# A feed-forward kernel with a gated GELU: transposes moved among the last products of a group, and the last product split by token halves

## The chip, the cores and the metric

One core of a Trainium2 chip. Its engines work side by side: TensorE makes matrix products and transposes, VectorE and ScalarE accumulate, copy and cast, and SyncE issues most loads and stores. The metric is the device time of one execution in microseconds (us), lower is better.

## The reference

```python
x: (8, 1024, 1024); w_gate, w_up: (1024, 4096); w_down: (4096, 1024)   # float32
gate = x @ w_gate
up = x @ w_up
gate = 0.5 * gate * (1 + tanh(sqrt(2 / pi) * (gate + 0.044715 * gate ** 3)))
out = ((gate * up) @ w_down).astype(float32)
```

## The kernel before

It works in 16-bit floats with fast matrix multiplication schemes, in eight passes over 1024 tokens. Two places matter: the first pair of column blocks (`first_pair`), where x and the first weights are just arriving, and the end of the last pass (`down_fast`), where a table `DOWN` says which product goes into which chain of sums in PSUM (the memory, in banks, that TensorE writes its results to) and which accumulates (`acc`) bring it to the output tiles.

The transposes of x in the first pair. TensorE writes eight blocks into one PSUM bank; VectorE copies one half of them out, then ScalarE the other half:

```python
    def x0_transpose(mh, g, b):
        h = x0_f16[:, mh * G + g]
        ps = ps_all[:, b].bitcast(FP16).rearrange("p (k m) -> p k m", m=P)
        for k in range(2 * KH):
            nc.tensor.transpose(ps[:, k], h[:, k * P : (k + 1) * P], identity)
        c = slice(g * P, (g + 1) * P)
        nc.vector.tensor_copy(xq["b11" if mh == 0 else "b12"][:, :, c], ps[:, 0:KH])
        if mh:
            nc.scalar.copy(xq["b22"][:, :, c], ps[:, KH : 2 * KH])
        else:
            return lambda: nc.scalar.copy(xq["b21"][:, :, c], ps[:, KH : 2 * KH])
```

The middle of the first pair (`x0_cast` is on VectorE, `cast_first` on ScalarE unless told otherwise, `outputs` uses both):

```python
        for kh in range(2):
            products(0, kh, slice(0, MH))
        for g in range(2):
            x0_cast(1, g)
        for g in range(2):
            x0_transpose(1, g, 6 + g)
        for g in range(2, G):
            x0_cast(1, g)
        outputs(0, 0)
        for w in range(2):
            cast_first(w, 0, slice(256, 512))

        nc.gpsimd.tensor_copy(mark, staging0(1, 0)[:, 0, 256:257])
        load_raw(0, 1)
        for kh in range(2):
            products(1, kh, slice(0, MQ))
        for g in range(2, G):
            x0_transpose(1, g, g - 2)
        outputs(0, 1)
        for w in range(2):
            cast_first(w, 1, slice(256, 512))
        for kh in range(2):
            products(1, kh, slice(MQ, MH))
```

The products and accumulates of the last stage, cut:

```python
        def product(e, js):
            _, entry, h, c, first = e
            lhs, rhs = place[h], q_chunk(entry)
            for j in js:
                for m in range(2):
                    nc.tensor.matmul(
                        ps_all[:, bank[c], m * MQ : (m + 1) * MQ],
                        lhs[:, j, m * P : (m + 1) * P],
                        rhs[:, j, :],
                        start=(first and j == 0 and m == 0),
                        stop=(j == NP - 1),
                        skip_group_check=True,
                    )
        ...
        for i, e in enumerate(DOWN):
            if e[0] == "mul":
                ...
                    product(e, range(NP))
                    for f in todo:      # the stores that wait behind a product
                        f()
                    todo.clear()
                ...
            elif e[0] == "acc":
                _, v, w, c, sc, st, o = e
                if v not in t:
                    t[v] = tmp_free.popleft()
                nc.vector.scalar_tensor_tensor(
                    tmp[:, t[v]], ps_all[:, bank[c]], float(sc * OSC), tmp[:, t[w]],
                    MUL, ADD if st > 0 else SUB,
                )
                if v != w:
                    used(w, i)
                if o >= 0:
                    def last(v=v, o=o):
                        store(v, o)
                        tmp_free.append(t.pop(v))

                    todo.append(last)
                if last_chain[c] == i:
                    ps_free.append(bank[c])
```

The table ends like this: (`'mul'`, entry, operand, chain, first) and (`'acc'`, to, from, chain, sign, sign, output block or -1). The accumulates of chain 6, which `mul 22` has ended, stand behind `mul 23`:

```python
    ('mul', 22, 'h5', 6, False),
    ('acc', 11, 11, 1, 1, -1, 1), ('acc', 5, 5, 1, -1, 1, -1), ('x',), ('x',),
    ('mul', 23, 'h1', 4, False),
    ('acc', 5, 5, 6, -1, 1, 5), ('acc', 7, 7, 6, 1, -1, 9), ('x',), ('acc', 8, 8, 4, 1, 1, 2),
```

## Time and profile before

| | before |
|---|---|
| device time, median of 3 (range) | 2263.22 us (2263.08 to 2264.55) |
| span of the profiled run | 2261.1 us |
| TensorE busy | 2247.4 us, 99% |
| TensorE waits for the copies of transposed x, first pair | 1.1 us in two waits |
| last matmul ends / last accumulate ends / span ends | 2256.80 / 2257.53 / 2261.10 us |

A line of the timeline has start, duration, engine, source line, operation, output<-input and shapes, and in brackets the idle time before it with what ended it. A line of the waits has who waited for what: total us, number, longest.

### The profile page before, as it was taken

What the parts mean: (1) busy time and instruction counts of PE and PEld (TensorE: products, weight loads), DVE (VectorE), ACT (ScalarE), POOL (GpSimd) and SP (SyncE); (2) the same over time, 40 slices, a digit from 0 to 9 for tenths busy, and PEclk for the clock granted to TensorE, in tenths of its full rate; (3) what the DMA queues carried; (4) which work ended last, traced back from release to release, by engine and by line L of the source; (5) the groups of instructions that cost most, each with busy time, mean ns of one, the idle gap of its engine ahead of it and who ended that gap; (6) DMA issues with size and microseconds to landing.
All of it is one profiled execution on the core that took longest, in us unless ns stands there. A gap on an engine that the chain in (4) does not pass through costs nothing.

```text
span 2261.1 us, 42805 instructions
## 1 busy us (share of the span) xinstructions
PE 2247.4 (99%) x16634; PEld 1624.9 (72%) x16634; DVE 1565.3 (69%) x2190; ACT 954.6 (42%) x1866; POOL 686.0 (30%) x825
## 2 busy tenths in 40 slices
PE   9999999999999999999999999999999999999999
PEld 4444444444444445888888888888888888888888
DVE  6676468884488755877776677766776667866674
ACT  4444135651266522665126550355404553055520
POOL 1342013330133300555115450245402543044520
PEclk9999999999999999999999999999999999999999
DMA  9997969989999999999998999988999889888876
GB/s 241 191 207 187 274 189 236 253 258 284 266 223 243 270 311 346 332 336 379 302 336 275 318 301 317 326 273 321 310 320 318 282 313 325 312 314 277 283 288 225
DMA packets 308093, 642.46 MB, mean 284 GB/s; under 512 B 79088, under 2 KB 185328, under 8 KB 287344
## 3 DMA queue, kind: packets, MB, share of 16 engines
q1 hardware_dynamic: 253104, 566.57, 73.0%
q0 software_dynamic: 54784, 73.14, 19.2%
q8 instruction: 130, 2.13, 0.4%
q14 instruction: 75, 0.61, 0.1%
HBM read 574.36 MB, written 138.41 MB: 315 GB/s over the span
## 4 chain that ended last, share of the span: by engine, by line
PE 84%; DVE 3%; DMA 2%; SPq 0%; issue 0%; ACT 0%; DVEq 0%
PE ps L848 40%; PE ps L1099 20%; PE ps L626 14%; PE ps L991 10%; DMA wd_quads<-x_sums 1%; DVE ring L351 1%; DVE h_s L278 1%; DVE tmp L645 1%; DMA w_ops<-h_s 1%; SPq L255 0%; DMA ring<-wd_ops 0%; DVE x_sums L278 0%; DVE h_a L663 0%; ACT ps L642 0%; DVE h_a L923 0%
## 5 line engine op out<-in xcount | busy, mean ns | idle before, releaser
L848 PEld LDWEIGHTS <-ring 128*128 128x128 f16 x8320 | 814.1, 98 | 94.4
L825 POOL TENSOR_TENSOR h_a<-tmp 128x256 f16<-128x256 f32 x640 | 468.8, 752 | 839.8 <-ACT tmp L813 832.3
L848 PE MATMUL ps<-x_sums,ring 128*128 128x256 f16 x5760 | 655.8, 273 | 0.0
L810 DVE TENSOR_TENSOR tmp<-tmp,ps 128x512 f32<-128x512 f32 x640 | 414.4, 683 | 146.9 <-PE ps L848 100.4
L626 PEld LDWEIGHTS <-ring 128*128 128x128 f16 x2632 | 257.4, 98 | 317.0 <-issue 8.2
L795 ACT COPY tmp<-ps 128x512 f32<-128x512 f32 x520 | 304.0, 585 | 237.7 <-PE ps L848 163.9
L626 PE MATMUL ps<-x_sums,ring 128*128 128x512 f16 x1504 | 342.1, 379 | 4.1 <-DVE tmp L645 2.2
L813 ACT ACTIVATE tmp<-tmp 128x256 f32<-128x256 f32 x640 | 263.8, 418 | 173.3 <-DVE tmp L808 79.7
L848 PE MATMUL ps<-x_b,ring 128*128 128x256 f16 x2560 | 305.6, 273 | 0.0
L808 DVE TENSOR_TENSOR tmp<-ps,tmp 128x512 f32<-128x512 f32 x240 | 165.4, 689 | 145.2 <-ACT tmp L795 101.0
L652 POOL TENSOR_TENSOR h_a<-tmp 128x512 f16<-128x512 f32 x94 | 151.6, 1613 | 374.7 <-ACT tmp L650 259.8
L626 PE MATMUL ps<-x_b,ring 128*128 128x512 f16 x1128 | 259.2, 379 | 0.0
L1099 PEld LDWEIGHTS <-h_a 128*128 128x128 f16 x2240 | 219.1, 98 | 25.4
L991 PE MATMUL ps<-ring,h_a 128*128 128x512 f16 x1024 | 222.3, 379 | 0.8 <-DMA ring<-wd_ops 0.8
L1099 PE MATMUL ps<-ring,h_a 128*128 128x256 f16 x1920 | 216.1, 273 | 0.0
L991 PEld LDWEIGHTS <-h_a 128*128 128x128 f16 x1152 | 112.7, 98 | 137.0 <-DMA ring<-wd_ops 1.3
L645 DVE TENSOR_TENSOR tmp<-ps,tmp 128x512 f32<-128x512 f32 x188 | 127.2, 683 | 107.0 <-ACT tmp L637 104.1
L1156 ACT ACTIVATE tmp<-ps 128x512 f32<-128x512 f32 x60 | 35.3, 597 | 362.6 <-PE ps L1099 274.6
L1168 DVE SCALAR_TENSOR_TENSOR tmp<-ps,tmp 128x512 f32<-128x512 f32 x120 | 81.1, 690 | 97.5 <-PE ps L1099 66.7
L637 ACT COPY tmp<-ps 128x512 f32<-128x512 f32 x188 | 110.0, 586 | 87.2 <-PE ps L626 84.4
L351 DVE TENSOR_TENSOR ring<-ring 128x1024 f16<-128x1024 f16 x188 | 133.1, 722 | 8.7 <-DMA ring<-in_w_up_dram 4.5
L1099 PE MATMUL ps<-ring,x_sums 128*128 128x256 f16 x1120 | 126.4, 273 | 0.0
(102 smaller groups left out, 1536.6 us busy)
## 6 DMA issues: line engine op xcount, KB each, us to landing
ring<-w_ops SPq DMA_DIRECT2D x480, 512.0 KB, 4.8
ring<-wd_quads SPq DMA_DIRECT2D x110, 1024.0 KB, 6.8
ring<-wd_ops SPq DMA_DIRECT2D x35, 1024.0 KB, 8.0
out_dram<-tmp SPq DMA_DIRECT2D x128, 256.0 KB, 6.5
w_ops<-h_s SPq DMA_DIRECT2D x128, 256.0 KB, 7.0
ring<-in_w_gate_dram POOLq DMA_DIRECT2D x23, 1024.0 KB, 10.2
ring<-in_w_up_dram POOLq DMA_DIRECT2D x23, 1024.0 KB, 17.9
wd_quads<-x_sums SPq DMA_DIRECT2D x131, 128.0 KB, 6.5
```

Source lines behind the costliest of these rows:

```text
L351: nc.vector.tensor_tensor(o, a, b, op)
L626: nc.tensor.matmul(ps(b, w), lhs[:, k], rhs[:, k, :], start=(first and k == 0), stop=(k == KH - 1), skip_group_check=True,)
L645: nc.vector.tensor_tensor(o, ps("b", w), o, ADD)
L652: nc.gpsimd.tensor_tensor(hq[TO[n]][:, i, :], tmp[:, t[n, 1]], tmp[:, t[n, 0]], MUL)
L795: nc.scalar.copy(tmp[:, t[o[1]]], ps_all[:, bank[o[2]]])
L808: nc.vector.tensor_tensor(d, b, a, SUB)
L810: nc.vector.tensor_tensor(d, a, b, ADD if o[4] == "add" else SUB)
L813: nc.scalar.activation(d, d, GELU, scale=GSC)
L825: nc.gpsimd.tensor_tensor(h, tmp[:, t[o[1]], MQ : 2 * MQ], g, MUL)
L848: nc.tensor.matmul(ps_all[:, bank[c], w * MQ : (w + 1) * MQ], lhs[:, w, k], rhs[:, k], start=(first and w == 0 and k == 0), stop=(k == KH ...
L991: nc.tensor.matmul(ps_all[:, bank[b, g]], lhs[:, j, g * P : (g + 1) * P], dc[:, n, :], start=(first and j == 0), stop=(j == NP - 1), skip_ ...
L1099: nc.tensor.matmul(ps_all[:, bank[c], m * MQ : (m + 1) * MQ], lhs[:, j, m * P : (m + 1) * P], rhs[:, j, :], start=(first and j == 0 and m ...
```

## The change

Its intent: TensorE should have products to do while the transposed x is copied out of PSUM, and the last accumulate and store should be half as long, with the first half done beside the second half's matmuls.

```diff
--- before.py
+++ after.py
@@ -1091,11 +1091,11 @@
                 ]
             )
 
-        def product(e, js):
+        def product(e, js, ms=range(2)):
             _, entry, h, c, first = e
             lhs, rhs = place[h], q_chunk(entry)
             for j in js:
-                for m in range(2):
+                for m in ms:
                     nc.tensor.matmul(
                         ps_all[:, bank[c], m * MQ : (m + 1) * MQ],
                         lhs[:, j, m * P : (m + 1) * P],
@@ -1127,8 +1127,35 @@
                 product(e, js)
         if p + 1 < NPASS:
             transpose_x(p + 1)
+
+        end = max(i for i, e in enumerate(DOWN) if e[0] == "mul") if p == NPASS - 1 else None
         count = 0
         for i, e in enumerate(DOWN):
+            if i == end:
+                finals = [f for f in DOWN[i:] if f[0] == "acc" and f[3] == e[3]]
+                for f in DOWN[i:]:
+                    assert f[0] != "snap" or f[2] != e[3]
+                for m in range(2):
+                    product(e, range(NP), (m,))
+                    if m == 0:
+                        for f in todo:
+                            f()
+                        todo.clear()
+                    c = slice(m * MQ, (m + 1) * MQ)
+                    for _, v, w, b, sc, st, o in finals:
+                        assert v == w and o >= 0
+                        nc.vector.scalar_tensor_tensor(
+                            tmp[:, t[v], c], ps_all[:, bank[b], c], float(sc * OSC),
+                            tmp[:, t[w], c], MUL, ADD if st > 0 else SUB,
+                        )
+                        r0 = p * TOK + o // 4 * MQ + m * P
+                        nc.sync.dma_start(
+                            out=out2[r0 : r0 + P, o % 4 * MQ : (o % 4 + 1) * MQ],
+                            in_=tmp[:, t[v], c],
+                        )
+                continue
+            if end is not None and i > end and e in finals:
+                continue
             if e[0] == "mul":
                 count += 1
                 if count > 2:
@@ -1191,18 +1218,17 @@
     def first_pair():
         bank = {(mh, j, w): 4 * mh + 2 * j + w for mh in range(2) for j in range(2) for w in range(2)}
 
-        def products(mh, kh, c):
-            for w in range(2):
-                for j in range(2):
-                    for k in range(KH):
-                        nc.tensor.matmul(
-                            ps_all[:, bank[mh, j, w], c],
-                            raw(0, 0)[:, w, kh * KH + k, j * P : (j + 1) * P],
-                            xq[f"b{kh + 1}{mh + 1}"][:, k, c],
-                            start=(kh == 0 and k == 0 and c.start == 0),
-                            stop=(kh == 1 and k == KH - 1),
-                            skip_group_check=True,
-                        )
+        def products(mh, kh, c, only=((0, 0), (0, 1), (1, 0), (1, 1))):
+            for w, j in only:
+                for k in range(KH):
+                    nc.tensor.matmul(
+                        ps_all[:, bank[mh, j, w], c],
+                        raw(0, 0)[:, w, kh * KH + k, j * P : (j + 1) * P],
+                        xq[f"b{kh + 1}{mh + 1}"][:, k, c],
+                        start=(kh == 0 and k == 0 and c.start == 0),
+                        stop=(kh == 1 and k == KH - 1),
+                        skip_group_check=True,
+                    )
 
         def outputs(mh, j):
             t = tmp_free.popleft()
@@ -1235,12 +1261,14 @@
             f()
         for w in range(2):
             cast_first(w, 1, slice(0, 256), nc.vector.tensor_copy)
-        for kh in range(2):
-            products(0, kh, slice(0, MH))
+        head, tail = ((0, 0), (0, 1), (1, 0)), ((1, 1),)
+        products(0, 0, slice(0, MH))
+        products(0, 1, slice(0, MH), head)
         for g in range(2):
             x0_cast(1, g)
         for g in range(2):
             x0_transpose(1, g, 6 + g)
+        products(0, 1, slice(0, MH), tail)
         for g in range(2, G):
             x0_cast(1, g)
         outputs(0, 0)
@@ -1249,10 +1277,11 @@
 
         nc.gpsimd.tensor_copy(mark, staging0(1, 0)[:, 0, 256:257])
         load_raw(0, 1)
-        for kh in range(2):
-            products(1, kh, slice(0, MQ))
+        products(1, 0, slice(0, MQ))
+        products(1, 1, slice(0, MQ), ((0, 0), (0, 1)))
         for g in range(2, G):
             x0_transpose(1, g, g - 2)
+        products(1, 1, slice(0, MQ), ((1, 0), (1, 1)))
         outputs(0, 1)
         for w in range(2):
             cast_first(w, 1, slice(256, 512))
```

## The prediction

> **What bounds the kernel now.** I read the page first (share of the engines, chain that ended last), then who waited for whom on TensorE, then the order of time in the first 30 us and in the last 30 us, because the change touches only these two places. The built programs of both kernels were compared too: the order of instructions on each engine, and what each waits on.
>
> ```profile
> span 2261.1 us, 42805 instructions
> ...
> PE 2247.4 (99%) x16634; PEld 1624.9 (72%) x16634; DVE 1565.3 (69%) x2190; ACT 954.6 (42%) x1866; POOL 686.0 (30%) x825
> ...
> PE 84%; DVE 3%; DMA 2%; SPq 0%; issue 0%; ACT 0%; DVEq 0%
> ```
>
> TensorE is busy for 99% of the span, at full granted clock, and carries most of the chain. 2261.1 - 2247.4 = 13.7 us without a matmul is all that any reordering can win, and it counts the very start and the very end. The waits of TensorE say which of it is in the middle:
>
> ```profile
> PE ps L626 <- DVE tmp L645: 2.2, 7, 0.4
> ...
> PE ps L1198 <- DVE x_b L305: 1.1, 2, 0.6
> PE ps L991 <- DMA ring<-wd_ops: 0.8, 1, 0.8
> ```
>
> The second line is the target of the first half of the change: twice, in the first pair, the products (L1198) wait for the copies that carry transposed x out of PSUM (L305). In order of time (start, duration, instruction, and the idle time before it):
>
> ```profile
> 17.39 0.69 DVE L297 TENSOR_SCALAR h_a<-h_a 128x1024 f16<-128x1024 f32 x1 [0.58 <-DMA h_a<-in_x_dram]
> ...
> 18.35 1.06 PE L303 MATMUL ps<-identity,h_a 128*128 128x128 f16 x16
> 19.07 0.86 DVE L305 COPY x_b<-ps 128x512 f16<-128x512 f16 x2 [0.98 <-PE ps L303]
> ...
> 19.99 3.65 PE L1198 MATMUL ps<-x_b,ring 128*128 128x256 f16 x32 [0.58 <-DVE x_b L305]
> ...
> 23.48 1.06 PE L303 MATMUL ps<-identity,h_a 128*128 128x128 f16 x16
> 24.12 0.87 DVE L305 COPY x_b<-ps 128x512 f16<-128x512 f16 x2 [2.30 <-PE ps L303]
> ...
> 24.48 1.04 ACT L331 CAST ring<-x_sums 128x1024 f16<-128x1024 f32 x1 [0.46 <-DMA x_sums<-in_w_up_dram]
> ...
> 25.05 3.65 PE L1198 MATMUL ps<-x_b,ring 128*128 128x256 f16 x32 [0.52 <-DVE x_b L305]
> ...
> 25.43 1.07 ACT L307 COPY x_b<-ps 128x512 f16<-128x512 f16 x2
> ```
>
> Sixteen transposes, two copies on VectorE, an idle TensorE, then products: this is seen at 18.35 and again at 23.48. The reader should also see the cast near the end of it: ScalarE casts weights at 24.48, when their load lands, and only then, at 25.43, makes its own copies of the second pair of transposes (the other half of x, L307). These are not held by TensorE but by a load. The end of the kernel, in order of time:
>
> ```profile
> 2246.16 10.64 PE L1099 MATMUL ps<-ring,h_a 128*128 128x256 f16 x96
> ...
> 2253.35 1.29 DVE L1168 SCALAR_TENSOR_TENSOR tmp<-ps,tmp 128x512 f32<-128x512 f32 x2 [2.15 <-PE ps L1099]
> 2256.84 0.69 DVE L1168 SCALAR_TENSOR_TENSOR tmp<-ps,tmp 128x512 f32<-128x512 f32 x1 [2.21 <-PE ps L1099]
> ```
>
> The last product ends at 2256.80, one accumulate of 0.69 us follows to 2257.53, then its store, whose landing and the closing waits take 2261.1 - 2257.53 = 3.57 us. The two accumulates at 2253.35 belong to the product before the last; in the kernel before they run while the last product is computed, and are over at 2254.64.
>
> **What the Trainium skill says.** "PSUM — Partial Sum Buffer", section "PSUM bank collisions raise a hardware error": the hardware does not arbitrate between two engines in one bank, and the rule is to guard PSUM by bank and not by address. The split of the last product meets it: the two halves are different columns of the same bank, so the half that is read by VectorE keeps TensorE out of the other. No instruction of the kernel before shows this; the built program after does (below). "PSUM — Partial Sum Buffer", section "Engine vs sequencer instructions": the queues of ScalarE and VectorE are strict FIFO. The trace agrees: the copies at 25.43 had had their transposes since 24.54, and stood behind the cast of 24.48. "DMA: Bandwidth & Descriptors", section "Anatomy of one DMA": some 2.0 us of each transfer are fixed, and mostly the receipt. The final stores here take 2.1 to 2.2 us from issue to landing, so halving one saves little.
>
> **The change part by part.** No work is added or removed on TensorE: both programs have 16,634 matmuls. VectorE has one instruction more, the queue one store more.
>
> First place, the head. Spacings from the trace: a 512-wide product (1.67 - 0.379) / 6 = 0.215 us for the seven at 28.54, a 256-wide one (3.65 - 0.273) / 31 = 0.109, a transpose (1.06 - 0.219) / 15 = 0.056. Four 512-wide products (0.86 us) now follow the transposes instead of preceding them. The transposes would start at 18.35 - 0.86 = 17.49; the cast of the first x tile has long ended, that of the second ends at 17.39 + 0.69 = 18.08 and holds its eight transposes until 18.14 (instead of 17.94). They issue until 18.59, the four products until 19.45. The copies on VectorE end at about 19.25, so the wait of 0.58 is gone and the next group starts at 19.45 instead of 19.99: 0.54 gained.
>
> Second place. 24 of the 32 products, the transposes, then 8 products of 0.109 = 0.87 us, more than the 0.52 waited. The group after it would start at 19.45 + (25.05 - 19.99) - 0.52 = 23.99, 1.06 earlier than before. But its 17th product needs ScalarE's two copies, in both programs. These stay at 25.43 to 26.50, since a load fixes the cast ahead of them. TensorE reaches that product at 23.99 + 16 x 0.109 = 25.73 and waits 0.8 us, to 26.56; before it came at 25.05 + 1.74 = 26.79 and did not wait. So of 1.06 us only 26.79 - 26.56 = **0.23 us** stays.
>
> Third place, the end, and here the order of the programs decides. The changed loop reaches the last product and issues both its halves with their accumulates at once; the two accumulates of the product before it, which stand behind the last product in the list, come later on VectorE: nine full accumulates, two halves, then two full ones. And the first matmul of the second half waits for VectorE's count of 2188, which by counting is the accumulate of the first half. Step by step: the 16th of the 32 products of 0.109 us starts at 2256.53 - 16 x 0.109 = 2254.79 and ends at 2255.06. VectorE starts 0.04 later, as it did at the end before, and takes about 0.42 us for 256 columns (an estimate: 0.69 less 256 elements at the 0.96 GHz that "VectorE: DVE Perf Modes", section "Specifications", gives; 0.27). At 2255.58 TensorE goes on instead of at 2254.89: a **new stall of 0.69 us**. Its last product ends at 2257.49, the half accumulate at 2257.95. Now the two displaced accumulates run, 0.60 us apart (1.29 for two, 0.69 for one): 2258.55 and 2259.16. The last store is issued after 2259.16 instead of after 2257.53: **1.63 us later**. It is again a full one of 256 KB, now closely behind another full one and a half one; at the 350 GB/s that the queue showed in its busiest slices these take 0.75 us each against 0.60 between their issues, so I add 0.15.
>
> Sum: -0.23 + 1.63 + 0.15 = +1.55 us on 2263.2.
>
> **The rivals.** A, the intent: both waits of the head vanish in full (-1.06) and the end is shortened by half an accumulate (-0.27) and some of the store: about -1.4, a time of 2261.8. For it speaks that both waits are in the trace; against it the order on VectorE and the wait for count 2188, which are in the built program, and the cast at 24.48. B, the head's gain is swallowed in full: TensorE waits 0.8 us at 282 us for a load of second weights; if that were fixed in time, a shift of 0.23 ahead of it would vanish, leaving +1.8, 2265.0. The chain shows this load hanging on stores and steps that follow TensorE from 233.6 us, so I think most of the shift passes. C, ScalarE's copies come sooner than I think, and the head keeps 1.06: then +0.7, 2263.9.
>
> **Range and chances.** The main reading gives 2264.8. The three runs before lie 1.5 us apart, as much as the effect itself, and B and C move it by +0.2 and -0.8; A is unlikely, as it needs the program to do otherwise than it was built. So I say 2264.7, 2263.0 to 2266.1. Two per cent are 45 us, more than all idle time of TensorE together: within 2% is as good as certain.
>
> **What would show it right or wrong.** Head: no wait of L305's copies ahead of the products at about 19.45 and 24.0, but a new wait of TensorE for ScalarE's copy of some 0.8 us at 25.7, and the first products of the second pair (L626) at about 28.3 instead of 28.54. End: a TensorE wait of about 0.7 us for VectorE in the middle of the last product; the last four VectorE instructions in the order half, half, full, full, the last of them ending some 1.7 us after the end of the last matmul (0.7 before), and the last store behind it. It would be wrong if the two full accumulates stood ahead of the halves, if TensorE did not stop between them, or if the loads at the head landed at other times.

## The result

| | before | changed |
|---|---|---|
| median of 6 (range) | 2263.05 us (2262.39 to 2264.55) | 2263.34 us (2262.54 to 2265.24) |
| ratio, 95% interval | | 1.0002, 0.9989 to 1.0015 |

A ratio is the mean time of one kernel's fast runs over that of the other's in the same rounds, so not quite the ratio of the medians. Nothing is to be seen in the whole time. The profiles show why: something was gained at the head and something lost at the end.

Timeline of the changed kernel, first pair (its products are L1224):

```profile
17.70 1.28 PE L303 MATMUL ps<-identity,h_a 128*128 128x128 f16 x16
...
18.82 3.65 PE L1224 MATMUL ps<-x_b,ring 128*128 128x512 f16 x28
...
21.68 1.05 ACT L331 CAST ring<-x_sums 128x1024 f16<-128x1024 f32 x1 [1.05 <-DMA x_sums<-in_w_gate_dram]
...
23.18 1.05 ACT L331 CAST ring<-x_sums 128x1024 f16<-128x1024 f32 x1 [0.45 <-DMA x_sums<-in_w_up_dram]
...
23.19 4.53 PE L1224 MATMUL ps<-x_b,ring 128*128 128x256 f16 x40
...
24.13 1.06 ACT L307 COPY x_b<-ps 128x512 f16<-128x512 f16 x2
...
27.56 3.75 PE L626 MATMUL ps<-x_b,ring 128*128 128x512 f16 x16
```

In the changed kernel's list of waits the two for L305 are gone: products run on without a gap from 18.82 and again from 23.19. The second pair (L626) starts at 27.56 instead of 28.54. And ScalarE's casts of the second halves of the weights, at 22.97 and 24.48 before, come at 21.68 and 23.18: the loads landed earlier, which the change does not ask for.

Timeline of the changed kernel, end (L1147 is the half accumulate, L1195 the full one):

```profile
2249.46 1.29 DVE L1195 SCALAR_TENSOR_TENSOR tmp<-ps,tmp 128x512 f32<-128x512 f32 x2 [2.86 <-PE ps L1099]
2254.65 0.42 DVE L1147 SCALAR_TENSOR_TENSOR tmp<-ps,tmp 128x256 f32<-128x256 f32 x1 [3.89 <-PE ps L1099]
...
2255.13 1.91 PE L1099 MATMUL ps<-ring,h_a 128*128 128x256 f16 x16 [0.52 <-DVE tmp L1147]
...
2257.07 0.42 DVE L1147 SCALAR_TENSOR_TENSOR tmp<-ps,tmp 128x256 f32<-128x256 f32 x1 [2.00 <-PE ps L1099]
2257.41 1.28 DVE L1195 SCALAR_TENSOR_TENSOR tmp<-ps,tmp 128x512 f32<-128x512 f32 x2
```

TensorE stops for 0.52 us between the halves, until VectorE has read the first. VectorE itself stood idle for 3.89 us before it, with two accumulates ready since about 2252.9 (chain 6); they come last, at 2257.41. Waits of TensorE in the changed kernel, the two lines that are new or other:

```profile
PE ps L991 <- DMA ring<-wd_ops: 1.0, 1, 1.0
...
PE ps L1099 <- DVE tmp L1147: 0.5, 1, 0.5
```

**Marks.** Whole times cannot part these effects, so each profile is read by marks. F is the start of the first product of the first pair (the arrival of the first loads moves it by 1.2 us from run to run), H the start of the second pair (L626), S its first product with summed x, and T the time from the start of the pair of accumulates that follows the third last product to the end of the span: 2261.10 - 2249.91 = 11.19 before, 2261.95 - 2249.46 = 12.49 changed (ends of the spans to a hundredth, from the trace; some expectations below work with 12.54, from the rounded 2262.0). The casts are counted from ScalarE's first cast.

| profile | F | gate cast | up cast | H - F | S - F | T |
|---|---|---|---|---|---|---|
| before | 11.43 | 12.64 | 14.15 | 17.11 | 20.69 | 11.19 |
| changed | 11.65 | 11.13 | 12.63 | 15.91 | 19.49 | 12.49 |
| head_only | 11.80 | 11.14 | 12.63 | 15.88 | 19.35 | 11.19 |
| end_only (old head) | 12.09 | 12.62 | 14.09 | 17.11 | 20.64 | 12.47 |
| order_fixed | 12.07 | 11.13 | 14.00 | 16.71 | 20.55 | 10.78 |
| two_banks | 12.31 | 11.14 | 14.00 | 16.73 | 20.56 | 10.15 |
| two_banks_again | 12.04 | 11.14 | 12.63 | 15.91 | 19.51 | 10.16 |
| after_again | 12.30 | 11.13 | 14.13 | 16.84 | 20.68 | 12.48 |
| casts_later | 12.00 | - | - | 15.91 | 20.34 | 10.18 |
| one_cast_later | 11.64 | 11.13 | - | 15.91 | 19.40 | 10.16 |
| fetch_early | 11.14 | 12.36 | 13.86 | 17.12 | 20.59 | 10.18 |
| loads_later | 11.98 | 15.22 | 16.73 | 19.44 | 23.27 | 10.99 |

A dash: the cast did not wait for its load there, so it tells nothing of it (by the load's completion marks, explained below, the up half had landed in time in both, 12.62 and 12.60 us after the first cast). Of loads_casts_later the marks are given with it.

### The profile page after: what moved, and what is told of

It reads as the page before. It is cut to its first block, busy times and chain, and to the rows that moved or that the text cites. A ratio compares the mean times of both kernels' runs of the same rounds, so it can differ in the third digit from the quotient of the medians.

```text
span 2262.0 us, 42808 instructions
## 1 busy us (share of the span) xinstructions
PE 2248.7 (99%) x16634; PEld 1625.5 (72%) x16634; DVE 1569.0 (69%) x2191; ACT 954.9 (42%) x1866; POOL 683.8 (30%) x825
## 3 DMA queue, kind: packets, MB, share of 16 engines
q8 instruction: 130, 2.13, 0.4%
## 4 chain that ended last, share of the span: by engine, by line
PE 83%; DVE 3%; DMA 2%; issue 1%; SPq 0%; ACT 0%; DVEq 0%; ACTq 0%
PE ps L848 40%; PE ps L1099 20%; PE ps L626 13%; PE ps L991 10%; DMA wd_quads<-x_sums 1%; DVE ring L351 1%; DVE h_s L278 1%; DVE tmp L645 1%; DMA w_ops<-h_s 1%; SPq L255 0%; DMA ring<-wd_ops 0%; DVE h_a L663 0%; DVE x_sums L278 0%; ACT ps L642 0%; DVE tmp L1147 0%
## 5 line engine op out<-in xcount | busy, mean ns | idle before, releaser
L626 PEld LDWEIGHTS <-ring 128*128 128x128 f16 x2632 | 257.3, 98 | 317.5 <-issue 8.7
L626 PE MATMUL ps<-x_sums,ring 128*128 128x512 f16 x1504 | 342.3, 379 | 4.3 <-DVE tmp L645 2.2
L626 PE MATMUL ps<-x_b,ring 128*128 128x512 f16 x1128 | 259.3, 379 | 0.0
L1195 DVE SCALAR_TENSOR_TENSOR tmp<-ps,tmp 128x512 f32<-128x512 f32 x119 | 80.4, 690 | 93.1 <-PE ps L1099 62.3
```

What stands on the lines that cost most here:

```text
L626: nc.tensor.matmul(ps(b, w), lhs[:, k], rhs[:, k, :], start=(first and k == 0), stop=(k == KH - 1), skip_group_check=True,)
```

## The experiments

Every kernel below gives the reference's result. Means are compared with the mean of the kernel before; medians are in us.

### One half of the change alone

head_only:

```diff
-        end = max(i for i, e in enumerate(DOWN) if e[0] == "mul") if p == NPASS - 1 else None
+        end = None
```

> The first pair as changed, the end as before. Two marks in the profile: H, the start of the first product of the second pair (L626; 28.54 us before, 27.56 after), and T, from the start of the pair of accumulates that follows the third last product to the end of the span (2261.1 - 2249.91 = 11.19 before, 2262.0 - 2249.46 = 12.54 after). My theory: the end is a loss of its own, so T is back at 11.2. For the head, theory L (a load decides): H is 27.6 if the second half of the gate weights lands early, as in the profile after (cast at 21.7), and 28.3 if it lands late, as in the profile before (cast at 23.0); where it lands is chance. Theory C (the change itself brings the loads forward): the cast is always at 21.7 with the changed head, H always 27.6. Whole time: 0.3 to 1.0 us under before, too little for the interval to show.

Median 2262.22, ratio 0.9995 (0.9981 to 1.0008), mean 1.1 us under before. T is 11.19 as before; H - F is 15.88, with both casts early.

end_only puts back the whole old `first_pair`:

```diff
-        products(0, 1, slice(0, MH), head)
+        for kh in range(2):
+            products(0, kh, slice(0, MH))
...
-        products(0, 1, slice(0, MH), tail)
(likewise in the second place)
```

> The end as changed, the first pair as before. My theory: T is 12.5 as after (+1.35), with a TensorE wait of 0.5 us for the first half's accumulate and two full accumulates behind the second half; whole time +1.35 us. Head: H 28.5 as before. Theory L: the cast of the second half of the gate weights may stand at 21.7 as well as at 23.0 with this unchanged head. Theory C: it stands at 23.0, as in the profile before.

Median 2263.84, ratio 1.0005 (0.9992 to 1.0017), mean 1.1 us over before. T is 12.47, and TensorE's wait for the first half's accumulate is 0.5. H - F is 17.11. So the two halves of the change are a gain and a loss that do not touch each other. The casts of the unchanged head stand at 12.62 and 14.09, just as before: in favour of theory C, the change does move a load.

### The end: is it the order or the bank?

order_fixed issues the accumulates of chain 6 ahead of the split product:

```diff
+        seq = list(DOWN)
+        if p == NPASS - 1:
+            n = max(i for i, e in enumerate(DOWN) if e[0] == "mul")
+            ahead_of = [e for e in DOWN[n:] if e[0] == "acc" and e[3] != DOWN[n][3]]
+            seq = DOWN[:n] + ahead_of + [DOWN[n]] + [e for e in DOWN[n + 1 :] if e not in ahead_of]
...
-        for i, e in enumerate(DOWN):
+        for i, e in enumerate(seq):
```

> As after, but the two accumulates of the product before the last stand ahead of the halves. Theory S (both the stall and the order cost): the wait of TensorE inside the last product stays at 0.5 (0.69 us from start to start), the last accumulate is a half (0.42 instead of 0.69) and the store behind it half as big (0.2 less): T = 11.19 + 0.69 - 0.27 - 0.2 = 11.4, still 0.2 over before. Rival O (the order alone is at fault, the stall costs little): T = 10.7.

Median 2262.0, ratio 0.9998 (0.9985 to 1.001). Timeline of order_fixed, end (L1152 is the half accumulate):

```profile
2252.85 1.29 DVE L1200 SCALAR_TENSOR_TENSOR tmp<-ps,tmp 128x512 f32<-128x512 f32 x2 [2.15 <-PE ps L1104]
...
2255.07 1.91 PE L1104 MATMUL ps<-ring,h_a 128*128 128x256 f16 x16 [0.51 <-DVE tmp L1152]
...
2257.02 0.42 DVE L1152 SCALAR_TENSOR_TENSOR tmp<-ps,tmp 128x256 f32<-128x256 f32 x1 [2.00 <-PE ps L1104]
```

The two full accumulates now run at 2252.85, beside the last product, and a half one ends the work. T is 10.78: the number of the rival O, but by another way, because the stall is still there in full (0.51). What I had mis-sized is what follows the last accumulate: 2260.20 - 2257.44 = 2.76 us here, 3.57 before. From the last accumulate to the last packet of its store it takes 1.39 us here and 1.81 before, 0.42 less (in the trace's packets 128 KB move in 0.52 us and 256 KB in 0.90); and from that packet to the end of the span 1.36 us here and 1.75 before, another 0.39. The sum, 0.69 stall - 0.27 accumulate - 0.42 - 0.39 = -0.39, meets the measured -0.41. The last of these four is no gain of the smaller store: head_only, with a full store, has 1.76 too, but the changed kernel, with a full store last, has 1.26. Most of it is one pause of SyncE, the engine that issues the stores: 0.33 to 0.34 us after its 2383rd instruction in the trace. In before, head_only, loads_later and loads_casts_later the pause stands there bare; in all other profiles SyncE waits at this same instruction for the landing of a store (0.67 to 0.90 us), and no pause shows beside it. Why it pauses there is open.

two_banks takes the bank away as a cause: the second half of the product goes into a free bank, and the sum that the old bank holds of it is added one product earlier, while nothing else needs VectorE.

```diff
+            m = max(i for i, e in enumerate(seq[:n]) if e[0] == "mul")
+            seq.insert(m, ("pre",))
...
+            if e[0] == "pre":
+                _, v, w, b, sc, st, _ = [f for f in seq if f[0] == "acc"][-1]
+                nc.vector.scalar_tensor_tensor(
+                    tmp[:, t[v], MQ:], ps_all[:, bank[b], MQ:], float(sc * OSC),
+                    tmp[:, t[w], MQ:], MUL, ADD if st > 0 else SUB,
+                )
+                continue
             if i == end:
+                b2 = ps_free.popleft()
...
-                    product(e, range(NP), (m,))
+                    if m == 1:
+                        bank[e[3]] = b2
+                    product((*e[:4], m == 1), range(NP), (m,))
```

> As order_fixed, but the second half of the last product goes into a free bank of PSUM, begun anew, and what its old bank holds of it is added by an extra half accumulate one product earlier. Theory S (the wait is one of bank, not of data): no wait of TensorE inside the last product, T = 11.19 - 0.27 - 0.2 = 10.7, the only end that beats the one before. Rival D (VectorE's order or its time sets the end whichever bank): T about 11.2 to 11.4. Head as head_only: H 27.6 with an early load, 28.3 with a late one.

Median 2260.72, ratio 0.999 (0.9978 to 1.0003), mean 2.2 us under before. Timeline of two_banks, end (L1144 is the early half accumulate, L1165 the two late ones):

```profile
2247.22 0.42 DVE L1144 SCALAR_TENSOR_TENSOR tmp<-ps,tmp 128x256 f32<-128x256 f32 x1 [0.66 <-ACT tmp L1201]
...
2254.59 0.42 DVE L1165 SCALAR_TENSOR_TENSOR tmp<-ps,tmp 128x256 f32<-128x256 f32 x1 [0.46 <-PE ps L1106]
...
2256.34 0.42 DVE L1165 SCALAR_TENSOR_TENSOR tmp<-ps,tmp 128x256 f32<-128x256 f32 x1 [1.32 <-PE ps L1106]
```

The same first half is read at 2254.59, and TensorE does not wait: its waits show nothing at the end. From the first half's accumulate to the second's it is 1.75 us, against 2.42 in order_fixed. T falls by 0.63 to 10.15, at the price of one more accumulate. So the stall was one of bank, not of data. What stops TensorE in the changed kernel is the wait for VectorE's count that stands in the built program and guards the bank; whether the chip would need it there was not tested. Of the 1.04 us by which T is now under before, 0.40 is the closing (1.36 instead of 1.75).

> The same kernel as two_banks once more, so that its gain over before has ten runs behind it: 1.5 to 2 us under before, T = 10.15, no TensorE wait inside the last product.

Median 2261.61, ratio 0.9994 (0.9982 to 1.0007), mean 1.3 us under before; T 10.16. The ten runs of this kernel lie between 2259.6 and 2262.5, the eighteen of before in the same calls between 2261.5 and 2265.8. This supports a gain of one to two us; neither interval excludes 1.

### The head: what does TensorE wait for, and what moves the loads?

The changed kernel once more:

> The changed kernel once more, beside the other two. T = 12.5 again. If where the up weights land is chance under the new head, this look shows either S - F = 19.5 (as in the profile after) or 20.55; the 16 KB fetch falls at 22.3 to 23.0 again. Whole time within 1 us of before.

Median 2263.48, ratio 1.0003 (0.999 to 1.0017), T 12.48. Timeline:

```profile
25.33 1.04 ACT L331 CAST ring<-x_sums 128x1024 f16<-128x1024 f32 x1 [1.96 <-DMA x_sums<-in_w_up_dram]
26.28 1.06 ACT L307 COPY x_b<-ps 128x512 f16<-128x512 f16 x2
...
27.40 1.91 PE L1224 MATMUL ps<-x_b,ring 128*128 128x256 f16 x16 [0.80 <-ACT x_b L307]
29.14 1.89 PE L626 MATMUL ps<-x_b,ring 128*128 128x512 f16 x8
```

This is the wait that the prediction describes (26.56 - 25.73 = 0.83 by its numbers): the up cast waits for its load, the copies stand behind the cast, and TensorE waits 0.80 us for them. H - F is 16.84, 0.27 under before, and S - F is 20.68, no gain at all. In the first look the up weights landed 1.5 us earlier, and the gain was 1.2 us. One kernel, two outcomes.

That a load decides was then forced. loads_later (on two_banks) adds two unneeded loads ahead of the second halves:

```diff
             for g in range(G):
                 x0_load(1, g)
+            for g in range(2):
+                nc.sync.dma_start(
+                    out=hf["s3"][:, 2048 * g + 2048 : 2048 * g + 4096].bitcast(FP32),
+                    in_=x2[g * P : (g + 1) * P, :],
+                )
```

> two_banks, with two loads of 512 KB that nobody needs put ahead of the second halves of the weights: these land some 2.6 us later. Theory L: ScalarE's copies of the second transposes go 2.6 us later with the casts, and TensorE waits 0.65 + 1.2 to 0.65 + 2.6 us for them; H - F = 18 to 19.3. Rival (transposes and copies set the head, the load has slack): wait and H - F as two_banks, 0.65 and 16.7.

One look, 2264.38. Timeline of loads_later:

```profile
28.56 1.06 ACT L307 COPY x_b<-ps 128x512 f16<-128x512 f16 x2
...
29.68 1.91 PE L1242 MATMUL ps<-x_b,ring 128*128 128x256 f16 x16 [3.39 <-ACT x_b L307]
```

The wait is 3.39 us, a little over the range I gave, and H - F 19.44. loads_casts_later, and casts_later without the extra loads, issue the two casts behind the copies:

```diff
-        for w in range(2):
-            cast_first(w, 0, slice(256, 512))
         ...
             x0_transpose(1, g, g - 2)
+        for w in range(2):
+            cast_first(w, 0, slice(256, 512))
```

> loads_later with the casts behind the copies as in casts_later. Theory L: the TensorE wait inside the last group of the first pair is gone although the loads are late; the lateness shows only where the second pair needs the weights (a wait ahead of or inside its first products, under 2 us), so that the copies stand at about 23.5 to 24.6 as soon as the transposes are through. Rival: the same wait as in loads_later.

One look, 2266.0. Timeline of loads_casts_later:

```profile
23.85 1.07 ACT L307 COPY x_b<-ps 128x512 f16<-128x512 f16 x2 [2.78 <-DVE x_b L305]
...
32.76 1.89 PE L626 MATMUL ps<-x_b,ring 128*128 128x512 f16 x8 [2.87 <-ACT ps L642]
```

The copies stand at 23.85, right behind the transposes, and H - F is 28.00 - 12.12 = 15.88 although the loads are nearly as late as in loads_later (casts 14.90 and 16.41 us after the first, 15.22 and 16.73 there). So the casts in front of the copies are the cause of that wait. But the lateness is only handed on: TensorE now waits 2.87 us in the second pair, for ScalarE's copies between banks (L642), which stand behind the same casts. I had said under 2.

> The end of two_banks; in the head, ScalarE's two casts of the second halves of the weights are issued after its copies of the second transposes, not before. Mark F: the start of the first product of the first pair (the launch jitters by up to 0.9 us, so H is read from F). So far H - F is 17.11 in both runs with the old head, 15.9 in two with the new head whose second up weights land early, 16.7 in two where they land 1.4 us late, with a TensorE wait of 0.65 for ScalarE's copy. Theory L (copies stand behind a cast that waits for a load): no such wait and H - F = 15.9 wherever that load lands. Rival: the copies are late for another reason, H - F = 16.7 when the load is late. T = 10.15 as two_banks. Whole time: the lowest so far or level with two_banks.

Median 2261.88, ratio 0.9995 (0.9981 to 1.0008). H - F is 15.91 as expected, but S - F is 20.34, for the same reason, in small. Since the up half landed in time in this look, it is no test of the theory (loads_casts_later is); beside looks with the same landing (changed, head_only and two_banks_again, S - F 19.35 to 19.51) the move cost 0.8 us or more. Timeline of casts_later:

```profile
30.62 1.89 PE L626 MATMUL ps<-x_b,ring 128*128 128x512 f16 x8 [0.82 <-ACT ps L642]
```

one_cast_later leaves the gate cast in its old place and moves the up cast alone:

```diff
-        for w in range(2):
-            cast_first(w, 0, slice(256, 512))
+        cast_first(0, 0, slice(256, 512))
         ...
             x0_transpose(1, g, g - 2)
+        cast_first(1, 0, slice(256, 512))
```

> two_banks, with only the second of ScalarE's two casts (up) put behind the copies of the second transposes; the first (gate) keeps its place ahead of them, where ScalarE has nothing else to do. Marks: F and H as before, S the start of the first product with summed x (second pair, L626). S - F is 20.7 in before, 19.4 to 19.5 where the up weights landed early under the new head, 20.55 where they landed late, 20.34 in casts_later, which moved the wait of TensorE for ScalarE from the copies (0.65) to the bank copies L642 of the second pair (0.8). Theory: both waits go, since ScalarE does one cast of 1.04 us less between the copies and L642: H - F = 15.9 and S - F = 19.5 whether up lands early or late. Rival (ScalarE is full there whatever the order): S - F stays at 20.3 or more. T = 10.15. Whole time: 2 to 2.5 us under before.

Median 2260.95, ratio 0.9991 (0.9978 to 1.0003), mean 2.1 us under before; H - F 15.91, S - F 19.40, T 10.16. Neither wait is there in this look, but with the up half in time the first would not be there either: S - F is that of two_banks_again (19.51), no more. Its span, 2257.3, is the shortest of all, in part because TensorE's wait for `wd_ops` at 282 us, 0.16 to 1.7 us in the others that have it, is missing here. Whether it holds with a late up load stays open.

What moves the load? Each load of 512 KB leaves 16 completion marks in the trace, and the last one counts ("DMA: Bandwidth & Descriptors", section "Why a DMA increments its semaphore by 16 and not by 1": the transfer is spread over up to 16 engines that finish independently). Among these loads every profile shows one transfer of another queue. The page of before:

```profile
q8 instruction: 130, 2.13, 0.4%
```

130 transfers, 2.13 MB: 16,384 bytes each. The Trainium skill, "Runtime: NRT & Kernel Launch", section "Instruction fetch mechanics", says that an engine's instructions are fetched in blocks of 16 KiB, 256 instructions, over its own DMA queue. TensorE has 16,634 matmuls and as many weight loads, 33,268 instructions or 130 blocks: the queue is TensorE's. DMA views of short windows show when the first fetch falls. Before, 20.6 to 21 us:

```profile
q8 instruction: 1, 0.02, 18.1%
```

Changed kernel, 22 to 22.5 us:

```profile
q8 instruction: 1, 0.02, 14.4%
```

In the trace's packets this first fetch takes 1.11 to 1.16 us. In the old head it falls at 20.7 (before) and 21.2 (end_only), while the gate half is landing; that one and all behind it are 1.5 us late. Each load is late by one completion mark only: in before, 15 of the gate half's 16 come 10.08 to 11.08 us after ScalarE's first cast and the last at 12.62.

In the new head it falls at 22.3 to 23.1: the gate half has landed before it in all of them, and of the six looks in which ScalarE waited for the up half, that was on time in three (changed, head_only, two_banks_again) and 1.4 to 1.5 us late in three (order_fixed, two_banks, after_again); by its completion marks it was in time in casts_later and one_cast_later too. What decides between these is open: from ScalarE's first cast the fetch begins at 11.7 to 11.9 us in all six. The completion marks narrow it down: where the up half is late, 15 of its 16 are there by 12.61, 12.60 and 12.36, and one comes at 13.97, 13.98 and 14.11; in changed and two_banks_again one mark of the load behind it is late instead (14.90 and 14.92). So it may hang on whether the DMA engine that carries the fetch has done its share of the up half by then; the trace does not name a packet's engine, so this is not shown. Nor does any run show why the new order makes the fetch later.

fetch_early tests whether the fetch is the cause by 64 more instructions of TensorE in the warm-up:

```diff
-        warm(9)
+        warm(7)
+        for _ in range(34):
+            nc.tensor.matmul(
+                ps_all[:, 0, 0:16], warm_w, warm_x[:, 0:16], start=True, stop=True
+            )
```

> two_banks with 32 more matmuls, nearly all tiny, in the warm-up (64 instructions of TensorE more), where TensorE waits for x anyway. In all six profiles a transfer of 16 KB on the queue of kind instruction falls at 20.7 to 23.0, and the load of weights in flight then lands 1.4 us late: the second gate half with the old head (fetch at 20.7 and 21.2), the second up half in order_fixed and two_banks (22.7 and 23.0). It is TensorE's own instructions (16,634 pairs at 64 bytes are the 2.13 MB of that queue). Theory F: with 64 instructions more the fetch comes some 3 us earlier, at about 17 to 19.5, hits a load of x with slack, and both second halves land on time: casts 11.13 and 12.63 us after the first cast, no TensorE wait for the copies, H - F = 15.9. Rival (the late landing has another cause): up cast still 14.0 after the first, H - F = 16.7.

One look, 2261.28. DMA view of fetch_early, 15 to 16 us:

```profile
q8 instruction: 1, 0.02, 6.9%
```

The fetch moved, to 15.0 us (I had said 17 to 19.5), and with it the first load that is late: x, whose first cast of the second half stands 7.14 us after ScalarE's first cast (5.79 before, 5.77 changed), and the gate and up casts at 12.36 and 13.86. That the fetch is TensorE's and makes loads late is shown, though by one look only: 64 instructions more of TensorE moved the fetch, and the first late load moved with it. The rest of theory F fell: an early fetch does not spare the weights but makes every later load late, and the head is back at H - F = 17.12 with new waits for x. In these profiles, the later the fetch, the fewer loads it held up.

## Why the prediction was right, point by point

The time lay in the range (2263.34 in 2263.0 to 2266.1), 1.4 us under the point; the sum had one term too large and one too small. That it lay there is partly luck and decides little: the interval of the ratio, -2.5 to +3.4 us, holds the main reading (+1.55), C (+0.7) and A (-1.4) alike. The marks decide, and they say that the end was right and the head was not: "if the loads at the head landed at other times" stands among the prediction's own signs of being wrong, and they did.

- **First place, 0.54 gained.** Right. From F, the second transposes start 22.30 - 11.65 = 10.65 us on instead of 23.48 - 11.43 = 12.05, that is 1.40 earlier: the 0.54, and 0.87 of products that now follow them. TensorE's small wait for the second x tile is there (0.2).
- **Second place, 0.23 kept of 1.06.** The mechanism is right: after_again has the wait (0.80, said 0.8) and the gain (0.27), and loads_later and loads_casts_later show the casts as the cause. But the step "these stay at 25.43 to 26.50, since a load fixes the cast ahead of them" failed: the landing is not fixed. With the changed order TensorE's instruction fetch fell behind the gate half in every look, and left the up half on time in some. With both early the head gains 1.2 us, five times the predicted term.
- **The stall of 0.69.** Right: the second half starts at 2255.13 after a wait of 0.52, or 0.69 by the weight loads, whose ends are not modelled. two_banks shows that the shared bank makes it.
- **The displaced accumulates, 1.63.** Right: from the marked pair to the end of the last accumulate it is 2258.69 - 2249.46 = 9.23 us instead of 2257.53 - 2249.91 = 7.62, so 1.61 more.
- **The store behind it, 0.15.** The queueing is right (from the last accumulate to the last packet 2.00 us instead of 1.81), though its 350 GB/s is the page's row for all queues, with 332 to 379 in the busiest slices. But the closing took 0.49 less (1.26 instead of 1.75), so T grew by 1.30 and not by 1.78: SyncE's pause of 0.34 is most of it, and the prediction had taken the closing as fixed. "Halving one saves little" measured 0.42 in order_fixed, and the 2.1 to 2.2 us of the final stores are 2.1 to 2.3 in the view.
- **The rivals.** A (the intent) did not come about. B (later waits swallow the head's gain): not in general. The wait at 282 us is 0 to 1.7 us whatever the head did, so it adds scatter of its own; loads_later, 2.7 us later at the head than two_banks, has no such wait left, but that took up no more than the 0.2 us that two_banks waits there. C (the full gain of 1.06 at the head) is what the first profile showed, for a reason that I had not seen.

In sum the changed kernel trades 0 to 1.2 us at the head for 1.30 at the end; the means of its six and five runs are 0.5 and 1.1 us over before.

## What to carry to other kernels

Before splitting a last product, ask two things of the built program: where the accumulates of the product before it now stand in the other engine's queue, and whether the two halves share a PSUM bank; a half that was to be read while the other was written needed a bank of its own here. A copy that TensorE needs should not stand in a queue behind a cast that waits for a load, and when such casts are moved back, look at what stands behind them in turn. Where loads set the start, read at which load the instruction fetch of TensorE falls: reordering a few instructions can move it.

## What the Trainium skill lacked or had wrong

- "Runtime: NRT & Kernel Launch", section "Instruction fetch mechanics", calls the cost of a block boundary mostly hidden. TensorE itself shows no wait there (before: its products run on over the fetch at 20.7), but loads beside it were held up: the first fetch of 16 KB took 1.11 to 1.16 us, and one of the 16 marks of a load of 512 KB beside it came 1.4 to 1.5 us late, and so did those behind it when the fetch fell early.
- No page says that the closing instructions on SyncE differ between nearly equal programs: from the last packet of the last store to the end of the span it took between 1.25 us (end_only) and 2.19 us (loads_later), where a pause of 0.33 to 0.34 us after SyncE's 2383rd instruction is bare in some and not seen in others.
- "PSUM — Partial Sum Buffer", section "PSUM bank collisions raise a hardware error", gives the rule but not its price: two halves of a product in one bank cost 0.69 us between them here, and a second bank took 0.63 us off the end.
